# One decoder layer with a hierarchical mixture of experts: two more weight slots, a reordered routing step and a reordered expert stage

## The chip, the cores and the metric

The kernel runs on one core of one Trainium2 chip. The metric is the device time of one execution in microseconds (us); lower is better. A core has five engines, each with its own in-order instruction queue: PE (matmul, with its weight loads shown as PEld), DVE (vector), ACT (scalar, activation functions), POOL (GpSimd) and SP, which here only issues transfers (DMAs). Transfers run on 16 shared DMA engines.

## What is computed

One layer on 256 tokens of width 1024 in f32: an RMS norm and a combined projection, two attention branches, an output projection added to `x`, and then a mixture of 32 experts, of which each token uses two out of one group of eight. Every expert's three weight matrices are 1 MiB each, so the expert stage reads 96 MiB whatever the routing says.

```python
h = rms_norm(x, norm_attn);  proj = h @ w_in
merged = sig(gA) * (A @ w_o_mla) + sig(gB) * (Bd @ w_o_dil)   # two attention branches
x = x + merged @ w_out
h2 = rms_norm(x, norm_ffn)
gp = softmax(h2 @ w_rg + b_rg);  g_p, g_i = top_1(gp)         # group of experts
e_p, e_i = top_2(softmax((h2 @ w_re + b_re)[g_i]))            # two experts inside it
combine = one_hot(g_i * 8 + e_i) * g_p * e_p / sum(e_p)
for e in range(32):
    he = silu(h2 @ w_gate[e]) * (h2 @ w_up[e])
    y += combine[:, e] * (he @ w_down[e])
x = x + y
```

## The kernel before

The tokens are two blocks (`tb` 0 and 1) of 128, one token per partition. Every large operand is an SBUF tile of 128 x 2048 f32 (1 MiB), called a slot.

**Projections** (`w_in`, `w_o_*`, `w_out`) stream through four slots `ring`. ACT and POOL (or DVE) split each weight into a high part `wh` and a low part `wl`, and PE sums three products into PSUM banks `pj`. A planner (`Weave`) holds prices of the engines and decides while the program is written in which order the attention branches' instructions stand between these matmuls.

**Experts** are worked off in eight groups of four (`g`), with 32 token places (`SLOT`) for each expert; what is over goes through `overflow`. `moe_loads` lists the 96 weight loads in the order w_gate, w_up, w_down of each group. `release` hands a slot back and calls `pump`, which issues the next load into the slot that came free first. All these loads stand in one queue, SP's, in the order of the program; each waits there until its slot is no longer read. The slots are four `early` (released at 40 us of the planner's clock, `first_slots`), eight `side`, four `ring`, `hT0`, `oT`, `late_slot`, and four `xs` that take the place of the projection's tiles, when `release(*extra_slots)` comes: 23 slots in all. The first loads into slots of group 0 are made in two halves (`release_halves`).

**Between the two stages** stands the routing. `x_out(tb, half)` adds the output projection to `x1` and sums its squares; `x_turn` transposes it for the router's matmul `logits`; `out_rms` makes 1/rms by an integer first guess and three Newton steps, on POOL for block 0 and on DVE for block 1; `x_sorted` copies `x1` into `tok`, reordered; `route` is ten dependent DVE steps per block that end in `sel`; `ranks` and `slots_of` count places on PE and DVE, `one_hot` builds the selection matrix, and `gather` and `gathered` bring the chosen tokens into `xg`. `warm_up` puts matmuls without use between them.

**One group** is: 32 matmuls of w_gate and 32 of w_up into one bank `gu`; `activate` (tanh on ACT, two products on DVE) to `he`; two transposes of the combine weights and two of `he` into `tr`, copied to `trs`; the next group's gather; then `down` (w_down, into `pd` or `px`), a copy to `do`, and `combine`, which adds into the four banks `y`. In group 0 four matmuls also add the residual `x1` to `y`. In the last group w_down comes in three column pieces (`PIECES`: 512, 256 and 256 columns, both rows of each partition), and each finished piece of `y` is copied to `x1` and sent out by ACT's and SP's queues.

All instructions of PE, DVE, ACT and POOL are recorded by one helper, `Engine`, so that they carry one line number, L128; tiles tell them apart. Loads of SP have lines of their own: L337 projections, L212, L215 and L217 experts, L228 halves.

Of the kernel before, what the change touches and what calls it, by code (L numbers as in the profile page):

```python
# [14 lines left out]
I32 = mybir.dt.int32  # L15
# [44 lines left out]
TUNE = dict(gap=0.103, dV=0.05, dS=0.208, dG=0.121, dPE=0.257, early=-0.366, norm=0.02, split1=-0.463, split2=1.641, pace=2.246, small=9.132, masks=18.02, busy=6, first=40.0, space=0.0, busy2=0, busy3=4, rms=1.0, sines=14.0, route=7, route2=6)  # L60
# [82 lines left out]
def layer(ctx, tc, A, out):  # L143
# [17 lines left out]
    x1 = ct([P, 2, D], "x1")  # L161
    late_slot = ct([P, 2048], "late_slot")
    NRING, NSIDE, NEARLY = 4, 8, 4
# [32 lines left out]

    def down_piece(t, piece):

        c0, n = piece
        return t[:, 2 * c0:2 * (c0 + n)].rearrange("p (j n) -> p j n", j=2)  # L200

    def pump():
        while moe_loads:
            name, e, piece = moe_loads[0]
# [6 lines left out]
            if piece is None:  # L211
                SP.dma_start(t, expert_src(name, e))  # L212
            elif name == "w_up":
                cut = slice(piece[0], sum(piece))
                SP.dma_start(t[:, cut], expert_src(name, e)[:, cut])  # L215
            else:
                SP.dma_start(down_piece(t, piece),  # L217
                             A[name][0, e].rearrange("(p j) n -> p j n", p=P)[:, :, piece[0]:sum(piece)])
# [18 lines left out]
    with ExitStack() as c1:  # L237
# [433 lines left out]
        biases = [wt([P, 512], f"bias{b}") for b in range(2)]  # L671
# [307 lines left out]

        tok = ct([P, 2, 8, P], "tok")  # L980
# [35 lines left out]
        def out_rms(tb, E):  # L1016

            y, (v, t) = rstd2[:, tb:tb + 1], (wt([P, 1], f"{name}{tb}") for name in ("rs_vo", "rs_to"))
            E.tensor_scalar(v, sso[:, tb, 0:1], sso[:, tb, 1:2], EPS, op0=ALU.add, op1=ALU.add)
            yield  # L1020
            E.tensor_scalar(y.bitcast(I32), v.bitcast(I32), -0.5, 1597463007.0, op0=ALU.mult, op1=ALU.add)
            E.tensor_scalar(v, v, -0.5, None, op0=ALU.mult)
            yield
            for _ in range(3):
                E.tensor_scalar(t, y, y, v, op0=ALU.mult, op1=ALU.mult)
                yield
                E.tensor_scalar(y, t, 1.5, y, op0=ALU.add, op1=ALU.mult)
                yield
# [419 lines left out]
    with ExitStack() as c2:  # L1448
# [3 lines left out]
        release(*extra_slots)  # L1452
# [8 lines left out]
        pc = ys[3][:, :NE]  # L1461

        def weights():
# [6 lines left out]
            S.activation(wts[:, :, 2], wts[:, :, 2], AF.Exp)  # L1470
            V.scalar_tensor_tensor(wts[:, :, 3], wts[:, :, 2], 1.0, wts[:, :, 1], op0=ALU.add, op1=ALU.mult)
# [12 lines left out]
        def count_full():  # L1484
            for tb in range(2):
# [15 lines left out]
        def overflow():  # L1501
# [6 lines left out]
            with tc.If(n > 0):  # L1508
                with tc.For_i(0, n, 1) as it:
# [11 lines left out]
                    for tb in range(2):  # L1521
# [14 lines left out]
                        activate(he, gus)  # L1536
# [16 lines left out]
        def activate(he, gu):  # L1553

            S.activation(he, gu[:, 0], AF.Tanh, scale=0.5)
            V.scalar_tensor_tensor(he, he, 1.0, gu[:, 0], op0=ALU.add, op1=ALU.mult)
            V.tensor_tensor(he, he, gu[:, 1], op=ALU.mult)

        def gather_all():

            for q in range(2):
                tag = "pd" if q else "px"
                px = ps2.tile([P, 4, P], F32, name=tag, tag=tag, bufs=1)
                for tb in range(2):
                    gather(px, q, tb)
                gathered(px, q)
# [11 lines left out]
        count_full()  # L1578
        ov = out.rearrange("b (t p) d -> p (b t) d", p=P)
        for g in range(NGRP):  # L1580
            final = g == NGRP - 1
            if g == 4:
# [107 lines left out]
```

## Time and profile before

| | |
|---|---|
| time, median of 3 runs | 503.06 us (501.61 to 507.61) |
| the profiled execution: its time | 503.13 us |
| its span, first to last instruction | 501.3 us |
| PE busy | 455.0 us (91%) |
| DVE, ACT, POOL busy | 201.5, 174.1, 237.3 us |
| read from HBM | 144.00 MB |
| mean granted TensorE clock | 0.986 of full speed |

The time is the device's; the span covers the instructions alone, so the two differ by 1.83 us in the profiled execution. A busy PE isn't a PE at its peak, since ends of pipelined matmuls are modelled.

### The profile page before, as it was taken

The page shows a single profiled execution, that of the slowest core. Times are in us where ns is not written, and L with a number is a line of the kernel's source. Part 1 is how long each engine was busy: PE and PEld are TensorE (multiplying, and loading weights), DVE is VectorE, ACT ScalarE, POOL GpSimd, SP SyncE. Part 2 cuts the span into 40 slices and gives each one's busy share as a digit, 9 for nine tenths or more (in the row PEclk, how much of TensorE's full clock was granted, in tenths as well). Part 3 has the DMA queues.
Part 4 walks back from the last instruction along what each step waited for, and adds up shares of the span by engine and source line. Part 5 has one row for each costly group of instructions (what it writes and reads, how often), then busy time and mean ns, then how long its engine had stood idle before and what let it go on. Part 6 is the DMA issues. An engine that isn't in the chain of part 4 may idle for free.

```text
span 501.3 us, 8356 instructions
## 1 busy us (share of the span) xinstructions
PE 455.0 (91%) x3254; PEld 324.9 (65%) x3254; DVE 201.5 (40%) x477; ACT 174.1 (35%) x334; POOL 237.3 (47%) x293
## 2 busy tenths in 40 slices
PE   7898889999999999999999999897988887868876
PEld 4796778877878888788888886362635443425322
DVE  6455986478633521473434176122212121212001
ACT  6765465646646654565444330000000000000001
POOL 5898878885778697567798650000000000000000
PEclk9999999998999999999999999999999999997989
DMA  8676946552534256278987986999999999999995
GB/s 283 234 224 201 412 131 215 175 165 84 160 101 159 93 167 202 82 227 332 374 303 281 418 341 242 424 418 420 420 419 420 422 418 421 422 418 422 413 385 173
DMA packets 43955, 145.61 MB, mean 290 GB/s; under 512 B 5752, under 2 KB 11402, under 8 KB 33162
## 3 DMA queue, kind: packets, MB, share of 16 engines
q1 hardware_dynamic: 43194, 144.53, 76.2%
q8 instruction: 26, 0.43, 0.4%
q10 hardware_dynamic: 720, 0.53, 0.3%
q14 instruction: 15, 0.12, 0.1%
HBM read 144.00 MB, written 1.05 MB: 289 GB/s over the span
## 4 chain that ended last, share of the span: by engine, by line
PE 50%; DMA 34%; DVE 7%; POOL 5%; issue 1%; ACT 1%; SPq 1%; POOLq 0%; DVEq 0%; ACTq 0%
PE pj L128 36%; DMA xs<-in_w_up_dram 10%; PE pt L128 6%; DMA side<-in_w_gate_dram 4%; DMA ring<-in_w_gate_dram 4%; DMA side<-in_w_up_dram 4%; DMA oT<-in_w_down_dram 4%; POOL wl L128 3%; PE s L128 3%; DMA ring<-in_w_down_dram 3%; DMA early<-in_w_down_dram 2%; PE y L128 2%; DMA early<-in_w_gate_dram 2%; DVE late_slot L128 2%; DMA ring<-in_w_in_dram 1%; PE pd L128 1%
## 5 line engine op out<-in xcount | busy, mean ns | idle before, releaser
L128 PE MATMUL pj<-wh,hT 128*128 128x512 f32 (+2 forms) x576 | 191.0, 394 | 2.0 <-ACT wh L128 1.5
L128 POOL TENSOR_TENSOR wl<-ring,wh 128x512 fp32r<-128x512 f32 (+1 forms) x124 | 156.5, 1288 | 44.7 <-ACT wh L128 44.4
L128 PEld LDWEIGHTS pj<-wh,hT 128*128 128x128 f32 x576 | 109.6, 192 | 22.2 <-issue 2.2
L128 PE MATMUL pj<-wl,hT 128*128 128x512 f32 (+2 forms) x288 | 110.9, 385 | 2.9 <-POOL wl L128 2.5
L128 ACT ACTIVATE wh<-ring 128x1024 fp32r<-128x1024 f32 (+2 forms) x78 | 79.3, 1018 | 81.3 <-PE pj L128 64.7
L128 POOL TENSOR_TENSOR wc<-wc,comb 128x128 f32<-128x128 f32 x16 | 6.0, 398 | 170.7 <-DVE wc L128 170.7
L128 PEld LDWEIGHTS pj<-wl,hT 128*128 128x128 f32 x288 | 55.5, 193 | 11.4 <-POOL wl L128 3.6
L128 PE MATMUL gu<-side,xg 128*32 128x256 f32 x416 | 43.8, 400 | 4.7 <-DMA side<-in_w_up_dram 4.6
L128 ACT ACTIVATE he<-gu 128x256 f32<-128x256 f32 x8 | 3.1, 384 | 123.2 <-PE gu L128 123.2
L128 PE MATMUL y<-do,trs 128*128 128x512 f32 x56 | 27.8, 618 | 11.7 <-DVE do L128 6.6
L128 DVE SCALAR_TENSOR_TENSOR he<-he,gu 128x256 f32<-128x256 f32 x8 | 3.4, 421 | 79.0 <-ACT he L128 79.0
L128 POOL TENSOR_TENSOR side<-side,st 128x512 f32<-128x512 f32 (+2 forms) x32 | 30.8, 991 | 5.9 <-DVE st L128 5.9
L128 PEld LDWEIGHTS gu<-side,xg 128*32 128x32 f32 x416 | 21.5, 115 | 17.2 <-DMA side<-in_w_up_dram 6.4
L128 PEld LDWEIGHTS y<-do,trs 128*128 128x128 f32 x56 | 9.5, 189 | 31.1 <-DVE do L128 12.9
L128 PE MATMUL gu<-ring,xg 128*32 128x256 f32 x176 | 25.1, 380 | 0.0
L128 DVE COPY do<-px 128x512 f32<-128x512 f32 x7 | 4.8, 691 | 50.3 <-PE px L128 50.3
L128 DVE COPY side<-pt 128x512 f32<-128x512 f32 (+2 forms) x26 | 16.6, 645 | 18.9 <-PE pt L128 17.7
L128 DVE TENSOR_TENSOR wl<-ring,wh 128x1024 fp32r<-128x1024 f32 (+2 forms) x16 | 18.7, 1168 | 12.3 <-ACT wh L128 11.9
L128 PE MATMUL gu<-xs,xg 128*32 128x256 f32 x160 | 19.4, 412 | 4.5 <-DMA xs<-in_w_up_dram 4.5
L128 ACT ACTIVATE do<-pd 128x512 f32<-128x512 f32 x7 | 4.2, 597 | 52.3 <-PE pd L128 52.3
L128 PE MATMUL pj<-wh,oT 128*128 128x512 f32 x64 | 21.1, 398 | 0.0
L128 DVE CUSTOM_DVE_ANT_0 side<-s,side 128x512 f32<-128x512 f32 (+2 forms) x32 | 15.4, 519 | 13.2 <-PE s L128 12.8
(270 smaller groups left out, 737.7 us busy)
## 6 DMA issues: line engine op xcount, KB each, us to landing
ring<-in_w_in_dram SPq DMA_DIRECT2D x25, 1024.0 KB, 5.2
side<-in_w_up_dram SPq DMA_DIRECT2D x16, 1024.0 KB, 17.6
side<-in_w_gate_dram SPq DMA_DIRECT2D x10, 1024.0 KB, 18.5
early<-in_w_gate_dram SPq DMA_DIRECT2D x7, 1024.0 KB
side<-in_w_down_dram SPq DMA_DIRECT2D x6, 1024.0 KB, 5.1
ring<-in_w_gate_dram SPq DMA_DIRECT2D x6, 1024.0 KB, 17.0
xs<-in_w_up_dram SPq DMA_DIRECT2D x6, 1024.0 KB
xs<-in_w_down_dram SPq DMA_DIRECT2D x6, 1024.0 KB, 18.4
```

The source lines that it names most:

```text
L128: r = f(*args, **kw)
```

## The change

- **Slots.** A fifth `early` slot is released with the four, and `x1` becomes a slot after the `xs`. For that `tok` takes over what `x1` was read for later: the residual (now added in group 2, from `tok` in its sorted order) and the staging of the output; the two gate-bias tiles become parts of `tok` as well.
- **Routing.** `out_rms` makes its first guess as exp(-0.5 ln(v)) on ACT and one Newton step on DVE, for both blocks. POOL copies block 0 to `tok` as soon as each half is there; ACT copies both halves of block 1. The block-0 route stands ahead of the block-1 route on DVE. `warm_up` has 3 + 5 matmuls in place of 6 + 7. ACT loads a table ahead of `x_out` and another after the exps of `weights`.
- **Groups.** w_gate and w_up go to two banks; the silu and the combine weights follow w_gate, ahead of w_up; the next group's gather is halved; `count_full` (two matmuls and DVE work on overfull experts) moves from ahead of group 0 to group 1.
- **Last group.** w_up is loaded in cuts of 1024, 512 and 512 columns and w_down in cuts of 1024 (the first row of each partition whole), 512, 256 and 256; the first row's matmuls run for all columns, then the second row's by pieces. `busy` puts 9 useless matmuls into w_up and 4 around the transposes.

Up to the last four halves of the output projection the order on PE, DVE, ACT and POOL is unchanged; on SP one load is added there.

```diff
-    NRING, NSIDE, NEARLY = 4, 8, 4
+    NRING, NSIDE, NEARLY = 4, 8, 5
...
+    UP = ((0, D), (D, 512), (D + 512, 512))
-    for half in range(2):
-        for j in range(4):
-            moe_loads.append(("w_up", NE - 4 + j, (half * 1024, 1024)))
-    for piece in PIECES:
-        for j in range(4):
-            moe_loads.append(("w_down", NE - 4 + j, piece))
-
+    for name, cuts in (("w_up", UP), ("w_down", UP[:1] + tuple((D + c0, n) for c0, n in PIECES))):
+        for c0, n in cuts:
+            for j in range(4):
+                moe_loads.append((name, NE - 4 + j, slice(c0, c0 + n)))
...
-        def out_rms(tb, E):
-
-            y, (v, t) = rstd2[:, tb:tb + 1], (wt([P, 1], f"{name}{tb}") for name in ("rs_vo", "rs_to"))
-            E.tensor_scalar(v, sso[:, tb, 0:1], sso[:, tb, 1:2], EPS, op0=ALU.add, op1=ALU.add)
-            yield
-            E.tensor_scalar(y.bitcast(I32), v.bitcast(I32), -0.5, 1597463007.0, op0=ALU.mult, op1=ALU.add)
-            E.tensor_scalar(v, v, -0.5, None, op0=ALU.mult)
-            yield
-            for _ in range(3):
-                E.tensor_scalar(t, y, y, v, op0=ALU.mult, op1=ALU.mult)
-                yield
-                E.tensor_scalar(y, t, 1.5, y, op0=ALU.add, op1=ALU.mult)
-                yield
+        def out_rms(tb):
+
+            y, (b, v, t) = rstd2[:, tb:tb + 1], (wt([P, 1], f"{name}{tb}") for name in ("rs_bo", "rs_vo", "rs_to"))
+            sum0, sum1 = sso[:, tb, 0:1], sso[:, tb, 1:2]
+            V.tensor_scalar(b, sum0, EPS, None, op0=ALU.add)
+            yield
+            S.activation(y, sum1, AF.Ln, bias=b)
+            S.activation(y, y, AF.Exp, scale=-0.5)
+            V.tensor_tensor(v, sum1, b, op=ALU.add)
+            yield
+            V.scalar_tensor_tensor(t, y, -0.5, y, op0=ALU.mult, op1=ALU.mult)
+            yield
+            V.tensor_tensor(t, t, v, op=ALU.mult)
+            yield
+            V.scalar_tensor_tensor(y, t, 1.5, y, op0=ALU.add, op1=ALU.mult)
...
+        nc.scalar.preload_act_table_set("natural_log_exp_and_others")
         half_unit(n_last, (0,))
         x_out(0, 0)
+        x_sorted(0, 0, G)
         half_unit(n_last + 1, (0,))
         x_out(0, 1)
+        x_sorted(0, 1, G)
         x_turn(0, 0)
         half_unit(n_last, (1,))
         x_out(1, 0)
         x_turn(0, 1)
-        rms0 = out_rms(0, G)
+        half_unit(n_last + 1, (1,))
+        rms0, rms1, r0, r1 = out_rms(0), out_rms(1), route(0), route(1)
+        next(rms0)
+        next(rms0)
+        x_out(1, 1)
+        x_turn(1, 0)
+        next(rms1)
+        logits(0, 0)
         for _ in rms0:
             pass
+        x_turn(1, 1)
+        next(rms1)
         for half in range(2):
-            x_sorted(0, half, G)
-        half_unit(n_last + 1, (1,))
-        x_out(1, 1)
-        x_turn(1, 0)
-        logits(0, 0)
-        x_turn(1, 1)
-        x_sorted(1, 0, G)
-        x_sorted(1, 1, S)
+            x_sorted(1, half, S)
         logits(0, 1)
         bank = pj_bank()
         lg[1], pp[1] = bank[:, :NR], bank[:, 64:64 + NE]
...
         warm_up(pxs[1], TUNE["route2"])
-        rms1, r0, r1 = out_rms(1, V), route(0), route(1)
+        next(r0)
+        for _ in rms1:
+            next(r0)
         for _ in range(4):
-            next(rms1)
-        for _ in rms1:
             next(r0)
         for _ in r0:
             next(r1)
...
-        release(*extra_slots)
+        release(*extra_slots, x1.rearrange("p t d -> p (t d)"))
...
@@ -1458,7 +1456,13 @@
         for bank in ("pd", "gu", "tr", "px"):
             ps2.tile([P, 512], F32, name=bank, tag=bank, bufs=1)
 
-        pc = ys[3][:, :NE]
+        def busy(n):
+
+            dst = ps2.tile([P, 512], F32, name="pd", tag="pd", bufs=1)
+            for _ in range(n):
+                PE.matmul(dst, ones, ones[:, None, :].to_broadcast([P, 4, P]), start=True, stop=True,
+                          skip_group_check=True)
+
...
-        count_full()
+            if g == 1:
+                count_full()
...
-            gu = ps2.tile([P, 2, FF], F32, name="gu", tag="gu", bufs=1)
-            for i, name in ((0, "w_gate"), (1, "w_up")):
+            gate = ps2.tile([P, 2, FF], F32, name="gu", tag="gu", bufs=1)[:, 0]
+            up = ps2.tile([P, 512], F32, name="px", tag="px", bufs=1)[:, :FF]
+            trs = w2([P, 4, P], "trs")
+            he = w2([P, 512], "do")[:, :FF]
+            for name, dst in (("w_gate", gate), ("w_up", up)):
...
+                        if final and dst is up and j and k in (4, 6):
+                            busy(2 if k == 4 else 1)
+                        PE.matmul(dst[32 * j:32 * j + 32], xg[:, k, 32 * j:32 * j + 32], w[j][:, k],
+                                  start=k == 0, stop=k == 7, skip_group_check=True, tile_position=(0, 32 * j))
...
-            if g + 1 < NGRP:
-                one_hot(g + 1)
-            he = w2([P, FF], "he")
-            wc = combine_weights(g)
-            activate(he, gu)
-            tr = ps2.tile([P, 4, P], F32, name="tr", tag="tr", bufs=1)
-            for tb in range(2):
-                PE.transpose(tr[:, 2 + tb], wc[:, tb].rearrange("p e s -> p (e s)"), ident)
-            if g + 1 < NGRP:
-                gather_all()
+                if dst is gate:
+                    silu(he, gate)
+                    tr = ps2.tile([P, 4, P], F32, name="tr", tag="tr", bufs=1)
+                    if g:
+                        weigh(g, tr, trs)
+                    if g + 1 < NGRP:
+                        one_hot(g + 1)
+            V.tensor_tensor(he, he, up, op=ALU.mult)
             hf = he.rearrange("p (q j) -> p q j", j=2)
+            if final:
+                busy(2)
+            else:
+                gather_half(1)
+            if g == 0:
+                weigh(g, tr, trs)
             for j in range(2):
                 PE.transpose(tr[:, j], hf[:, :, j], ident)
-            trs = w2([P, 4, P], "trs")
-            V.tensor_copy(trs, tr)
+            if final:
+                busy(2)
+            V.tensor_copy(trs[:, :2], tr[:, :2])
+            if not final:
+                gather_half(0)
             dos = {}
-            if g == 0:
+            if g == 2:
                 for tb in range(2):
                     for half in range(2):
...
+                        PE.matmul(ys[2 * tb + half], ident,
+                                  tok[:, tb, :, half * 64:(half + 1) * 64].rearrange("p r q -> p q r"), start=False,
...
+            def down(bank, piece, jfs, start):
+
                 c0, n = piece
-                tag = "px" if i == 1 else "pd"
+                for jf in jfs:
+                    for j in range(4):
+                        w = at("w_down", j).rearrange("p (j n) -> p j n", n=D)[:, jf, c0:c0 + n]
+                        PE.matmul(bank[32 * j:32 * j + 32, c0 % 512:c0 % 512 + n], trs[:, jf, 32 * j:32 * j + 32], w,
+                                  start=start and jf == 0, stop=jf == 1, skip_group_check=True,
+                                  tile_position=(0, 32 * j))
...
-            pieces = PIECES if final else WHOLE
-            down(0, pieces[0])
-            if not final:
-                combine(pieces[0])
-            down(1, pieces[1])
+                    V.tensor_copy(do, src)
+
             if final:
-                combine(pieces[0])
-                combine(pieces[1])
-                down(2, pieces[2])
-            combine(pieces[-1])
+                banks = [ps2.tile([P, 512], F32, name=tag, tag=tag, bufs=1) for tag in ("pd", "px")]
+                for half in range(2):
+                    down(banks[half], WHOLE[half], (0,), True)
+                for i, piece in enumerate(PIECES):
+                    bank = banks[piece[0] // 512]
+                    if i == 2:
+                        combine(PIECES[0])
+                    down(bank, piece, (1,), False)
+                    rows_out(i, bank, piece)
+                combine(PIECES[1])
+                combine(PIECES[2])
+            else:
+                for i, (piece, tag) in enumerate(zip(WHOLE, ("pd", "px"))):
+                    bank = ps2.tile([P, 512], F32, name=tag, tag=tag, bufs=1)
+                    down(bank, piece, (0, 1), True)
+                    rows_out(i, bank, piece)
+                    combine(piece)
```

SP at the start of the expert stage, the loads that fill the slots ahead of group 0's halves (L212 and L228), before; the number behind a tile's name tells tiles of one name apart:

```order
L212 DMA ring_63<-in_w_up_dram 128x2048
L212 DMA xs_2640<-in_w_up_dram 128x2048
L212 DMA xs_2641<-in_w_down_dram 128x2048
L212 DMA xs_2642<-in_w_down_dram 128x2048
L212 DMA xs_2643<-in_w_down_dram 128x2048
L228 DMA early_78<-in_w_down_dram 128x1024
L228 DMA early_79<-in_w_gate_dram 128x1024
L228 DMA early_80<-in_w_gate_dram 128x1024
```

and now (L209 and L221; x is `x1`, `hT` and `ring` come ahead of these rows in both):

```order
L209 DMA ring_63<-in_w_up_dram 128x2048
L209 DMA ring_64<-in_w_up_dram 128x2048
L209 DMA xs_2634<-in_w_down_dram 128x2048
L209 DMA xs_2635<-in_w_down_dram 128x2048
L209 DMA xs_2636<-in_w_down_dram 128x2048
L209 DMA xs_2637<-in_w_down_dram 128x2048
L209 DMA x_58<-in_w_gate_dram 128x2048
L221 DMA early_79<-in_w_gate_dram 128x1024
```

One load more, into `x1`, stands between the `xs` and the halves, and what the `xs` hold has moved on by one matrix.

DVE in the routing, from block 0's group choice (`pen`) to the sum that selects its experts (`sel`), before:

```order
L128 TENSOR_TENSOR pen<-iota_u,gidx 128x4
L128 SCALAR_TENSOR_TENSOR el_lg<-pen,el_lg 128x32
L128 SCALAR_TENSOR_TENSOR el_lg<-pj,rstd_157,rbias 128x36
L128 MAX top<-el_lg 128x8
L128 MAX gtop<-el_lg 128x8
L128 MAX_INDEX idx<-top,el_lg 128x8
L128 MAX_INDEX gidx<-gtop,el_lg 128x8
L128 TENSOR_TENSOR pair<-iota_u,idx 128x64
L128 TENSOR_TENSOR pen<-iota_u,gidx 128x4
L128 TENSOR_TENSOR sel<-pair 128x32
```

and now:

```order
L128 TENSOR_TENSOR pen<-iota_u,gidx 128x4
L128 SCALAR_TENSOR_TENSOR el_lg<-pen,el_lg 128x32
L128 MAX top<-el_lg 128x8
L128 MAX_INDEX idx<-top,el_lg 128x8
L128 TENSOR_TENSOR pair<-iota_u,idx 128x64
L128 SCALAR_TENSOR_TENSOR el_lg<-pj,rstd_157,rbias 128x36
L128 TENSOR_TENSOR sel<-pair 128x32
```

Block 1's steps (`gtop`, `gidx`, the second `pen`) no longer stand between those of block 0.

PE in the last group, the end of the second down piece to the last piece's matmuls, before (`y` are the output banks, `xg` the copied piece):

```order
L128 MATMUL px<-early_81,trs 32x256
L128 MATMUL y_2648<-xg,trs 128x512
L128 MATMUL y_2650<-xg,trs 128x512
L128 MATMUL y_2649<-xg,trs 128x256
L128 MATMUL y_2651<-xg,trs 128x256
L128 MATMUL pd<-early_78,trs 32x256
L128 MATMUL pd<-early_79,trs 32x256
L128 MATMUL pd<-early_80,trs 32x256
L128 MATMUL pd<-early_81,trs 32x256
```

and now:

```order
L128 MATMUL px<-xs_2634,trs 32x256
L128 MATMUL y_2643<-xg,trs 128x512
L128 MATMUL y_2645<-xg,trs 128x512
L128 MATMUL px<-hT_2438,trs 32x256
L128 MATMUL px<-ring_63,trs 32x256
L128 MATMUL px<-ring_64,trs 32x256
L128 MATMUL px<-xs_2634,trs 32x256
L128 MATMUL y_2644<-xg,trs 128x256
L128 MATMUL y_2646<-xg,trs 128x256
```

The second piece's two matmuls into `y` have moved behind the last down piece, which has four matmuls in place of eight.

## Rows read from the trace of the kernel before

**Rows 1.** The page, DMA share and GB/s in 40 slices of the span

```profile
DMA  8676946552534256278987986999999999999995
GB/s 283 234 224 201 412 131 215 175 165 84 160 101 159 93 167 202 82 227 332 374 303 281 418 341 242 424 418 420 420 419 420 422 418 421 422 418 422 413 385 173
```

**Rows 2.** The chain that ended last: start us, us, engine and what

```profile
326.55 13.42 DMA ring<-in_w_down_dram
...
483.40 3.25 PE gu L128 x26
...
491.68 1.05 PE px L128 x10
492.73 2.78 PE y L128 x8
495.50 1.05 PE pd L128 x16
...
497.01 1.15 PE y L128 x4
498.18 0.42 DVE x L128
```

**Rows 3.** Windows: stretch, its length, busy PE, PEld, DVE, ACT, POOL, PEclk, DMA share, GB/s

```profile
70.00:75.00 5.00, 5.00 (x25) 4.24 (x24) 3.70 (x7) 3.15 (x8) 5.00 (x5) 1.00 0.35 92
289.00:292.00 3.00, 3.00 (x24) 2.69 (x23) 1.72 (x4) 1.78 (x4) 2.33 (x7) 1.00 0.44 128
302.00:306.00 4.00, 4.00 (x69) 2.72 (x71) 2.82 (x13) 0.77 (x5) 0.00 (x0) 1.00 0.09 24
360.00:400.00 40.00, 33.25 (x350) 17.09 (x352) 8.03 (x22) 1.58 (x3) 1.51 (x4) 1.00 1.01 420
```

**Rows 4.** Timeline of SP's queue: start us, us, line, what is issued

```profile
46.12 2.28 SPq L212 DMA_DIRECT2D early<-in_w_gate_dram  x4
57.15 66.78 SPq L337 DMA_DIRECT2D ring<-in_w_in_dram  x11
...
304.71 0.33 SPq L228 DMA_DIRECT2D early<-in_w_down_dram  x1
```

**Rows 5.** Windows of 1 us in the last group, columns as in rows 3

```profile
476.00:477.00 1.00, 1.00 (x21) 0.49 (x13) 0.00 (x0) 0.00 (x0) 0.00 (x0) 1.00 1.03 410
485.00:486.00 1.00, 1.00 (x9) 0.36 (x2) 0.00 (x0) 0.00 (x0) 0.00 (x0) 0.50 1.07 372
489.00:490.00 1.00, 0.68 (x8) 0.29 (x12) 0.26 (x1) 0.00 (x0) 0.00 (x0) 1.00 0.99 324
493.00:494.00 1.00, 1.00 (x3) 0.38 (x2) 0.19 (x1) 0.12 (x1) 0.00 (x0) 1.00 0.21 73
```

**Rows 6.** Timeline of routing and first gate: start us, us, engine, operation [idle before]

```profile
286.17 0.63 ACT L128 ACTIVATE xg<-x 128x512 f32<-128x512 f32 x1 [3.66 <-DVE x L128]
...
291.99 0.98 PE L128 MATMUL s<-wr,xT 128*128 128x36 f32 x8
...
292.24 3.27 POOL L128 COPY tok<-x 128x512 f32<-128x512 f32 x3
...
293.38 0.25 DVE L128 SCALAR_TENSOR_TENSOR el_lg<-s,rstd,rbias 128x36 f32<-128x36 f32 x1
...
294.45 1.11 DVE L128 SCALAR_TENSOR_TENSOR el_lg<-pen,el_lg 128x32 f32<-128x32 f32 x1
...
296.42 0.19 DVE L128 TENSOR_TENSOR sel<-pair 128x32 fp32r<-128x32 f32 x1
296.53 0.18 DVE L128 SCALAR_TENSOR_TENSOR el_lg<-pen,el_lg 128x32 f32<-128x32 f32 x1
...
302.77 3.66 PE L128 MATMUL gu<-early,xg 128*32 128x256 f32 x64
```

**Rows 7.** Groups of instructions on ACT: busy us, mean ns | idle before

```profile
L128 ACT ACT_TABLE_LOAD x2 | 2.6, 1283 | 0.0
```

**Rows 8.** DMA issues: count, KB each, median us from issue to landing

```profile
out_dram<-x SPq DMA_DIRECT2D x2, 128.0 KB, 1.7
```

More of the change, by code (lines that the diff above doesn't have):

```diff
@@ L57, in split_const @@
     return parts
-TUNE = dict(gap=0.103, dV=0.05, dS=0.208, dG=0.121, dPE=0.257, early=-0.366, norm=0.02, split1=-0.463, split2=1.641, pace=2.246, small=9.132, masks=18.02, busy=6, first=40.0, space=0.0, busy2=0, busy3=4, rms=1.0, sines=14.0, route=7, route2=6)
+TUNE = dict(gap=0.103, dV=0.05, dS=0.208, dG=0.121, dPE=0.257, early=-0.366, norm=0.02, split1=-0.463, split2=1.641, pace=2.246, small=9.132, masks=18.02, busy=6, first=40.0, space=0.0, busy2=0, busy3=4, rms=1.0, sines=14.0, route=5, route2=3)
 class Weave:
@@ L161, in layer @@
     x1 = ct([P, 2, D], "x1")
+    tok = ct([P, 2, 8, P], "tok")
     late_slot = ct([P, 2048], "late_slot")
-    NRING, NSIDE, NEARLY = 4, 8, 4
+    NRING, NSIDE, NEARLY = 4, 8, 5
     ring = [ct([P, 2048], f"ring{i}") for i in range(NRING)]
@@ L670, in layer @@
         bias_t = {}
-        biases = [wt([P, 512], f"bias{b}") for b in range(2)]
+        biases = [tok[:, 0, 4 * b:4 * b + 4].rearrange("p r q -> p (r q)") for b in range(2)]
         def gate_bias(b, half):
@@ L1484, in count_full @@
         def count_full():
+            pc = ps2.tile([P, 512], F32, name="pd", tag="pd", bufs=1)[:, :NE]
             for tb in range(2):
@@ L1551, in overflow, with silu, gather_half, weigh @@
             release(*ws)
[L1553 to L1563, printed above, removed]
-                for tb in range(2):
-                    gather(px, q, tb)
-                gathered(px, q)
+        def silu(he, gate):
+            S.activation(he, gate, AF.Tanh, scale=0.5)
+            V.scalar_tensor_tensor(he, he, 1.0, gate, op0=ALU.add, op1=ALU.mult)
+        def gather_half(q):
+            tag = "pd" if q else "px"
+            px = ps2.tile([P, 4, P], F32, name=tag, tag=tag, bufs=1)
+            for tb in range(2):
+                gather(px, q, tb)
+            gathered(px, q)
+        def weigh(g, tr, trs):
+            wc = combine_weights(g)
+            for tb in range(2):
+                PE.transpose(tr[:, 2 + tb], wc[:, tb].rearrange("p e s -> p (e s)"), ident)
+            V.tensor_copy(trs[:, 2:], tr[:, 2:])
         def combine_weights(g):
@@ L1628, in combine @@
                 for tb in range(2):
-                    PE.matmul(yv[tb], trs[:, 2 + tb], dos[piece], start=False, stop=final, skip_group_check=True)
+                    PE.matmul(yv[tb], trs[:, 2 + tb], dos[piece], start=g == 0, stop=final, skip_group_check=True)
                 if final:
                     sl = slice(c0, c0 + n)
-                    S.activation(x1[:, 0, sl], yv[0], AF.Copy)
-                    V.tensor_copy(x1[:, 1, sl], yv[1])
-                    nc.scalar.dma_start(ov[:, 0, sl], x1[:, 0, sl])
@@ L1635, in combine @@
-                    SP.dma_start(ov[:, 1, sl], x1[:, 1, sl])
-            def down(i, piece):
-                c0, n = piece
-                tag = "px" if i == 1 else "pd"
+                    S.activation(yo[:, 0, sl], yv[0], AF.Copy)
+                    V.tensor_copy(yo[:, 1, sl], yv[1])
+                    nc.scalar.dma_start(ov[:, 0, sl], yo[:, 0, sl])
+                    SP.dma_start(ov[:, 1, sl], yo[:, 1, sl])
+            def down(bank, piece, jfs, start):
+                c0, n = piece
+                for jf in jfs:
[4 more added lines that the diff above has]
+                                  tile_position=(0, 32 * j))
@@ L1640, in down, with rows_out @@
+            def rows_out(i, bank, piece):
+                c0, n = piece
                 do = xg.rearrange("p k t -> p (k t)")[:, c0:c0 + n] if final else w2([P, 512], "do")
                 dos[piece] = do
-                pd = ps2.tile([P, 512], F32, name=tag, tag=tag, bufs=1)
-                for jf in range(2):
-                    for j in range(4):
-                        w = at("w_down", j)
-                        w = down_piece(w, piece) if final else w.rearrange("p (j n) -> p j n", n=D)[:, :, c0:c0 + n]
-                        PE.matmul(pd[32 * j:32 * j + 32, :n], trs[:, jf, 32 * j:32 * j + 32], w[:, jf],
-                                  start=jf == 0, stop=jf == 1, skip_group_check=True, tile_position=(0, 32 * j))
+                src = bank[:, c0 % 512:c0 % 512 + n]
```

35 lines of the change are left out of this document (12 added, 23 removed).

## The prediction

> **What bounds the kernel now.** I read the page's slices first. In the last 40% of the span the DMA line is all nines, at about 420 GB/s, while the slices before it swing between 82 and 418 [rows 1]. Next the chain of waits: from 326.55 to 483.4 us it is transfers alone, each released by the one before, and only then PE, ACT and DVE of the last group [rows 2]. In that stretch PE is busy 33.25 of 40 us at full clock while the transfers stand at 1.01 of their engines [rows 3]: the expert stage waits for its weights. So I looked for holes in the transfers. The one that matters lies ahead of the stage: from 302 to 306 their share is 0.09 [rows 3], because all 23 slots are full and SP can issue only when group 0's first matmuls let a slot go, at 304.71 [rows 4]; bytes flow 1.3 us later. From there arithmetic sets the end: 73 loads of 1 MiB are left, at 2.5 us each (1.049 MB by 420 GB/s). A load made before 302 is worth 2.5 us; an earlier release is worth what it is earlier, as long as a hole is left. Behind this stands the tail: the last w_up lands at 483.4 and the end comes 17.9 us later, by a chain of computation, though w_down's traffic ends near 493.9, where the DMA share has fallen to 0.21 [rows 2, 5].
>
> **The fifth early slot: 2.5 us.** Its load is issued at about 48 us behind the other four [rows 4]; it costs SP one issue of some 0.5 us and the transfers 2.5 us, in a stage with room (share 0.35 from 70 to 75 us [rows 3]). Queued behind it on SP is the next `ring` load, which waited for its slot until 57.15 anyway [rows 4]; four ring slots stand between a load and its use, so I take zero, with 2.5 us as the upper end if the ring ran dry.
>
> **The slot in `x1`: 2.5 us.** It is free when ACT's copies to `tok` end, which I place at 293.4 to 295.7, behind ACT's Ln and Exp. Its load stands on SP behind the `xs` and ahead of the halves, so it carries the transfers from about 302.2 to 304.7, into the hole. Were the copies 7 us later it would hold up the halves queued behind it. Ends: 0 and 2.5; I take 2.5, since the hole is 3.8 us wide.
>
> **Routing: 0.65 us.** Block 0's selection `sel` came at 296.42 [rows 6]. One step ahead of it shows a cost that goes: masking block 0's logits took 1.11 us and ended with POOL's three copies (292.24 + 3.27 = 295.51), while the same step for block 1, after them, took 0.18 [rows 6]. Now POOL is through with its copies before 289: 0.9 us less. Against it, block 0's router matmuls end only at 292.97 [rows 6], so the faster 1/rms moves the first `el_lg` just from 293.38 to about 293.05; and block 1's Newton step waits for ACT's Exp near 293.4, with block 0's DVE steps queued behind that wait. Walking DVE's new order at 0.2 us per dependent step gives `sel` at 295.75, 0.65 earlier. Block 1 no longer runs between block 0's steps and ends later, so its gather gains only 0.5; the count matmuls in front of the first gate are gone. First gate matmul: 302.1 in place of 302.77 [rows 6]; first release 304.05. Ends: -0.4 (block 1 bound by ACT) and 1.2. The transfers then run to 304.7 and start again at 305.35: a hole of 0.65 stays, so these three terms add, and no more than 0.65 is left to win here. The first table load (1.28 us [rows 7]) lies in 3.66 us of idle ACT [rows 6]; the second has from about 304 until the gate's end near 305.8.
>
> A rule bears on the moved copies. The Trainium skill (SBUF — State Buffer, "SBUF: two separate sides") says that DVE and GpSimd have a port pair in common which one of them holds for a whole instruction, and that of DVE's operations only those with two SBUF inputs or in a two-port mode compete for it. The masking step reads two SBUF tiles and waited; `el_lg` at 293.38, from PSUM, took 0.25 beside the same copies [rows 6]: the trace agrees. The copies now stand beside `x_out`, which reads PSUM and one SBUF tile: nothing by the rule; were one `x_out` held up as the masking step was, it would be 0.9 late and the sum up to 0.65 smaller.
>
> **Experts' groups: 0.** Four residual matmuls, `count_full` and the silu move inside stages where PE has 6.7 idle us in 40 [rows 3]; the transfers hide that. If this cover were gone, see the third rival.
>
> **Tail: 0.55 us.** The rates of the last windows are 410 GB/s with cuts of 1024 columns, 372 with 512, 324 with 256 [rows 5]. w_up's second half, now in 512s, lands 0.5 later. w_down needed 10.5 us behind the last w_up (483.4 to 493.9); by those rates its old cuts make 12.1 (2.1 MB at 372, 2.1 at 324) and the new ones 11.15 (2.1, 1.05, 1.05), so I scale 10.5 to 9.7. The same scaling puts the old second piece at 491.1; PE got it at 491.68 [rows 2], so 0.6 is added for the signal. With 5.65 from the terms above, the last w_up lands at 483.4 - 5.65 + 0.5 = 478.25, w_down's second column piece 8.3 + 0.6 later at 487.15, the last at 488.55. The work between (some 5 matmuls, product, transposes, copy, first rows) is done by about 483.5 at full clock and waits for w_down. From 487.25 PE bounds: four matmuls of 256 columns 0.53 (half of 1.05), `y` of the first piece 1.7 and of the second 0.85 (with start-up 2.78 together), last piece 0.53, its `y` 1.15 [rows 2]: 492.0. Copy and wait 0.45, then 2.7 us from the copy's end to the span's end as before (498.6 to 501.3 [rows 2]): 495.1. Ends: -0.3 and 1.9 (PE waits for nothing).
>
> **Sum.** 2.5 + 2.5 + 0.65 + 0.55 = 6.2; 501.3 - 6.2 = 495.1. The profiled execution took 1.83 us more than its span, and its 503.13 stands at the median of the runs (503.06): **496.9 us**, 1.2% faster. A change of 2%, about what a measurement of this kernel can tell from no change, would be 10 us.
>
> **Rivals.** *No hole for `x1`*: its copies or the `xs` come late, or the release does, and the second slot and the routing give nothing: 3.15 us back, 500.1. For it: nearly all of the gain there is to be had in 4 us of one window. Chance 0.14.
>
> *Half clock in the tail.* After PE had waited for w_up its clock was 0.50 at 485 [rows 5], that is 1.2 GHz. The filling matmuls speak against it, the waits for w_down's cuts for it. With the PE terms doubled the first rows are ready at 486.4, the end comes at 500.7, the time is 502.5. Chance 0.1.
>
> *Slower: PE becomes the bound of the expert stage.* One group's weights take 30 us, PE's work about 25. w_up's bank is now also that of a gather and of the second down piece, and `do` holds the silu's result too: each reuse makes PE or ACT wait for a reader. From 5 us more per group on, every further one counts seven times: 2 us over is 14 against 6.2 gained, 510.9. Against it: the first 5 us are free, and the clock was full [rows 3]. Chance 0.04.
>
> *Small cuts signal later.* A 128 KB transfer took 1.7 us from issue to landing [rows 8], 0.3 of it bytes. If each of w_down's cuts signals 1.4 behind its traffic in place of 0.6, PE's last stretch starts 0.8 later: 497.7. Chance 0.08. The Trainium skill (DMA: Bandwidth & Descriptors, "Anatomy of one DMA") gives about 2.0 us of fixed cost for a transfer, most of it between the last byte and the signal; by that, an estimate, the time is 498.3. No row here shows the fixed cost by itself.
>
> *More than forecast.* Routing gains 1.3, the hole closes, and PE waits for nothing in the tail: 501.3 - 5 - 1.3 - 1.9 = 493.1, time 494.9; 492.6 if the gap at 289 to 292 (share 0.44 [rows 3]) closes as well. Chance 0.08.
>
> **How the numbers follow.** The forecast keeps 0.56; its own range is 495.3 to 498.3. To hold 8 in 10 the range takes in late signals and the lost slot, with a margin for the spread of runs: 493.5 to 500.7. Faster by over 2% 0.07; slower by over 2% 0.04; within 2% 0.89.
>
> **What would show it.** Right: 25 loads issued ahead of the first half-load, at most 1 us without transfers before 306, nines from then on, the last w_up landing near 478, the first gate matmul near 302.1, PEclk 1.0 from 478 on. Wrong: the masking step still at 1 us, a hole of 3 us, w_up landing as before, PE busy above 29 of 30 us in a group, or an end more than 17 us behind the last w_up.

## The result, and the profile after

| | kernel before | changed kernel |
|---|---|---|
| time, median | 503.11 us (14 runs) | 506.5 us (14 runs, 504.1 to 509.31) |
| ratio to the kernel before | | 1.0057, 95% interval 1.0032 to 1.0083 |
| profiled execution: time, span | 503.13, 501.3 us | 504.1, 502.3 us |
| mean granted TensorE clock | 0.986 | 0.986 |

The change made the kernel 0.6% slower, where 1.2% faster was forecast; 506.5 lies above the range. Every ratio below is to the kernel before on the same chip, so that kernels are compared by their ratios; 0.01 is 5 us. One execution of no_fill (1150.26 us) and one of wc_early (579.1 us) were far longer than all others of their kernels and are in neither the ratios nor the medians below.

The page of the changed kernel, TensorE's clock and the transfers in 40 slices, answers to [rows 1]:

```profile
PEclk9999999999999999999999998999999989999989
DMA  8676966553524267268987999999999999999972
GB/s 285 230 224 204 419 201 216 174 168 114 144 86 166 88 187 238 77 236 326 373 294 291 402 358 359 423 421 419 420 420 421 418 421 418 421 419 417 340 273 84
```

The sixth slice (201, before 131) has the fifth early load, and the hole ahead of the expert stage is smaller (25th slice: 359, before 242; from 300 to 305 us the share is 0.92). So the two loads came in where they were forecast, and the routing ends earlier: the first gate matmul runs at 299.50 in place of 302.77, the first half-load goes out at 301.44 in place of 304.71 [rows 4, 6]. Some 1.7 us of this is not the change's (see the routing below). Timelines of DVE (the masking step of block 0, then `sel`), PE and SP of the changed kernel:

```profile
292.60 0.19 DVE L128 SCALAR_TENSOR_TENSOR el_lg<-pen,el_lg 128x32 f32<-128x32 f32 x1
...
293.66 0.18 DVE L128 TENSOR_TENSOR sel<-pair 128x32 fp32r<-128x32 f32 x1
...
299.50 0.85 PE L128 MATMUL gu<-early,xg 128*32 128x256 f32 x12
...
301.44 1.89 SPq L221 DMA_DIRECT2D early<-in_w_gate_dram  x3
```

What was gained there is gone by the end of the last group. The chain that ended last was transfers from 326.55 to 483.4 us in the kernel before [rows 2]. In the changed kernel the chain, which reaches back some 100 us, holds no transfer: it is PE's own order, with ACT, DVE and POOL in its waits. Its last group (start us, us, what):

```profile
471.86 3.63 PE gu L128 x64
...
475.51 0.39 ACT do L128
...
475.93 0.42 DVE do L128
476.35 0.21 DVE wc L128
...
476.69 0.41 POOL wc L128
...
477.15 0.33 PE tr L128
...
477.83 3.60 PE px L128 x34
481.44 0.95 PE pd L128 x2
482.39 0.55 PE px L128 x2
482.94 0.67 PE pd L128 x2
...
488.18 0.98 PE px L128 x10
489.16 0.66 PE pd L128 x2
...
499.16 0.42 DVE tok L128
```

w_gate ends at 475.5, and then PE stands until 477.15: the transposes of the combine weights `wc` come next in its queue. `wc` needs nothing of w_gate, but its comparison stands in DVE's queue behind the silu, which waits for tanh on ACT, and POOL's product follows the comparison. Then w_up takes 11.3 us (477.83 to 489.16), where the 64 matmuls of the group before took 3.59. PE's waits, by what ended them (us in all, times, longest), of the changed kernel and then of the kernel before:

```profile
PE tr L128 <- POOL wc L128: 13.9, 8, 1.8
PE y L128 <- DVE do L128: 7.0, 7, 1.3
PE y L128 <- ACT do L128: 5.0, 7, 0.7
...
PE tr L128 <- DVE trs L128: 0.5, 1, 0.5
```

```profile
PE pd L128 <- DVE trs L128: 7.7, 7, 1.1
PE y L128 <- DVE do L128: 6.6, 7, 1.0
PE y L128 <- ACT do L128: 5.1, 7, 0.8
PE gu L128 <- DMA side<-in_w_up_dram: 4.6, 3, 1.9
PE gu L128 <- DMA xs<-in_w_up_dram: 4.5, 5, 1.9
```

The wait for `trs` (1.1 in each of seven groups) was changed for one of 1.7 to 1.8 for `wc`, and no wait for an expert's load is left. How full an engine that sets the end looks, is seen in one group of each kernel (windows, columns as in [rows 3]), of before and then of after; the later rows are on the clock:

```profile
349.85:371.64 21.79, 18.96 (x205) 10.30 (x204) 4.71 (x12) 0.98 (x2) 0.76 (x2) 1.00 1.01 419
...
450.00:455.00 5.00, 2.78 (x19) 0.98 (x23) 0.00 (x0) 0.00 (x0) 0.00 (x0) 0.50 1.02 423
```

```profile
425.50:449.00 23.50, 19.64 (x209) 10.36 (x212) 4.87 (x13) 0.98 (x2) 0.76 (x2) 1.00 1.01 420
...
478.00:480.00 2.00, 2.00 (x32) 1.09 (x25) 0.29 (x1) 0.00 (x0) 0.00 (x0) 0.65 1.02 418
480.00:482.00 2.00, 2.00 (x12) 0.81 (x4) 0.00 (x0) 0.00 (x0) 0.00 (x0) 0.50 1.04 399
```

In the group of before PE waited for no load at all, and yet was busy 18.96 of 21.79 us: the other 2.83 are waits for its own results (`trs` 1.15, `do` 0.72 and 0.96), and transfers cover none of that. 21.8 us is PE's own pace. With it the stretch from the first to the last gate can be parted. Before: 302.77 to 473.11, 170.3 us, of which PE's pace makes 25.3 (group 0, with the residual) and six times 21.8, in sum 156.1; 14.2 us are left, the room that the loads leave PE (below: the cover). Waits that loads ended are 9.4 of it; the rest stands between and behind these waits, where w_up's matmuls ran two at a time and the clock fell (0.50 from 450 to 455 us). After: 299.50 to 471.79, 172.3 us, with no wait for a load. The 16.2 above 156.1 are 3.5 in the residual's matmuls (7.07 us for 3.60), 3.4 at the half clock (windows at 310 and 405 with 0.66 and 0.69), and 9.3 in the groups, 1.3 each.

So PE came to the last w_up at 477.8, just when its last cut landed (issued at 471.48; loads of w_up in that stretch took 5.7 to 6.3 us in the median). The transfers ended just behind 487 us (share 0.10 from 487 to 488, then none; the last piece was forecast for 488.55), but nothing waited for them any more, and 24.5 us of tail stood behind 477.8.

### The profile page after: what moved, and what is told of

Read it like the earlier page. It is cut to its first block, busy times and chain, and to the rows that moved or that the text cites. A ratio compares the mean times of both kernels' runs of the same rounds, so it can differ in the third digit from the quotient of the medians.

```text
span 502.3 us, 8374 instructions
## 1 busy us (share of the span) xinstructions
PE 461.7 (92%) x3254; PEld 325.4 (65%) x3254; DVE 204.2 (41%) x486; ACT 178.4 (36%) x341; POOL 233.6 (47%) x283
## 5 line engine op out<-in xcount | busy, mean ns | idle before, releaser
L128 ACT ACTIVATE do<-gu 128x256 f32<-128x256 f32 x8 | 3.1, 384 | 75.5 <-PE gu L128 64.8
L128 PE MATMUL px<-side,xg 128*32 128x256 f32 x160 | 28.4, 399 | 0.0
L128 ACT ACTIVATE side<-side,st 128x512 f32<-128x512 f32 (+2 forms) x32 | 18.4, 578 | 4.4 <-DVE st L128 4.4
L128 DVE SCALAR_TENSOR_TENSOR do<-do,gu 128x256 f32<-128x256 f32 x8 | 3.4, 421 | 38.9 <-ACT do L128 38.9
L128 PE MATMUL tr<-ident,wc 128*128 128x128 f32 x16 | 5.2, 328 | 14.1 <-POOL wc L128 13.9
L128 PE MATMUL s<-side,side 64*128 64x128 f32 (+2 forms) x160 | 15.9, 294 | 0.9 <-DVE st L128 0.8
```

Of the source, the lines that this page charges most:

```text
L128: r = f(*args, **kw)
```

## Experiments

**Theory 1**: the new wait, with the residual, brings PE to the last w_up so late that nothing covers the tail, whose fills and clock then count. **Theory 2**: the fills of the tail alone. **Theory 3**: the transfers (new cuts, new slots).

**no_fill.** The changed kernel without `busy`:

```diff
-                        if final and dst is up and j and k in (4, 6):
-                            busy(2 if k == 4 else 1)
...
-            if final:
-                busy(2)
-            else:
+            if not final:
                 gather_half(1)
...
-            if final:
-                busy(2)
```

> The changed kernel (504.1 us in its profile) without the 13 filling matmuls of the last group. Theory 1 (PE itself sets the end now: the wait for the combine weights ahead of w_up and the residual's strided read hold PE up in every group, so that it comes to the last w_up no earlier than its weights land, at 477.8, and the fills then stand in the path): PE still starts the last w_up near 477.8, w_up ends near 482 in place of 489.2, the end comes some 6.5 us earlier: 497 to 498. Theory 2 (the fills alone, the wait is harmless): the same 497 to 498. Theory 3 (PE waits for transfers: the new cuts or slots): PE only waits instead, 504.

500.71 us, ratio 0.9942 (0.992 to 0.9964): 1.1% or 5.8 us below the changed kernel, against theory 3. (The times expected of no_fill, weigh_late, resid and slots23 count from the profiled execution's 504.1, 2.4 below the median, so it is differences that compare: here 6.5 us were expected.) PE still starts w_up at 477.74 and now waits 0.5 us each for `do` and `trs` and 0.4 for the first copied piece; the fall of the clock at 475 to 485 stays. In the chain of the changed kernel the eight pieces of fills are 4.7 us. Besides, a fill parts the matmuls of the four column strips, which otherwise run side by side: two between fills take 0.55, 64 in a row 3.59, and the 30 behind the first fill take 2.5 us more than their part of that. Less the 1.4 of waits that the fills covered these are 5.8 of the 6.1 by which the spans differ (502.3 and 496.2).

**weigh_late.** The transposes go behind w_up; the products of the combine weights stay:

```diff
-                    if g:
-                        weigh(g, tr, trs)
+                    wc = combine_weights(g)
...
-            if g == 0:
-                weigh(g, tr, trs)
+            weigh(wc, tr, trs)
```

> The changed kernel with the two transposes of the combine weights behind w_up and the half gather, as its group 0 has them; their products stay where they are on DVE and POOL. Theory 1: the wait of 1.7 to 1.8 us for POOL goes from seven groups, PE's group takes 21.8 us as before in place of 23.1, PE comes to the last w_up some 9 us earlier and waits there for the weights, which land near 477.5; the fills run inside that wait, and the end comes near 493.5 in the span, time 495. Theory 2: the fills still cost their 6 us, only the last wait counts: 502. Theory 3: 504.

496.23 us, ratio 0.9867 (0.9822 to 0.9913): 1.9% below the changed kernel, with all fills in place. Its gates come 21.8 us apart (321.40, 343.19), as in the kernel before. The chain of weigh_late is again one of transfers up to the last group, and PE's timeline shows it waiting for w_up in the last two groups; no window of 5 us up to 490 is below full clock:

```profile
436.25 19.72 DMA side<-in_w_down_dram
...
456.03 15.00 DMA side<-in_w_up_dram
471.03 0.04 issue
471.07 1.92 PE px L128 x28
```

```profile
446.09 3.64 PE L128 MATMUL px<-early,xg 128*32 128x256 f32 x58 [1.85 <-DMA early<-in_w_up_dram]
...
469.78 0.62 PE L128 MATMUL px<-ring,xg 128*32 128x256 f32 x2 [0.18 <-DMA ring<-in_w_up_dram]
471.07 0.40 PE L128 MATMUL px<-side,xg 128*32 128x256 f32 x1 [0.67 <-DMA side<-in_w_up_dram]
```

w_up ends at 480.42, 8.7 us earlier than with the wait; the span is 494.5, where 493.5 was expected here and the prediction's sum gave 495.1.

**wc_early.** PE's order is untouched, but the products are written ahead of the group's w_gate, so that nothing is left to wait for:

```diff
             at = lambda name, j: moe_at[name, 4 * g + j]
+            wc = combine_weights(g)
...
-                        weigh(g, tr, trs)
+                        weigh(wc, tr, trs)
```

> The changed kernel with PE's order untouched, the combine weights' transposes between w_gate and w_up as the change has them, but their products written ahead of the group's w_gate, so that DVE and POOL are through with them before PE comes there. If it is the wait for POOL that costs (theory 1), PE's group falls from 23.1 to some 21.3 us, transfers set the end and the time is that of weigh_late: 495.5 to 497. If the place itself costs (a break between w_gate and w_up, or the waits that follow), 501 or more.

498.09 us, ratio 0.9912 (0.9883 to 0.9941): 1.4% below the changed kernel, 1.1 us above theory 1's range, with an interval that meets that of weigh_late. The wait for `wc` is left once (0.94 us, group 1), a group takes 21.3 us (371.33 to 392.60), and the place in PE's queue costs nothing that is clear of the noise: the wait does. Coming earlier only lengthens the waits for loads (2.3 in weigh_late for the first row here), and behind them the clock is at 0.50 from 445 to 450 in its profile:

```profile
PE px L128 <- DMA early<-in_w_up_dram: 3.8, 3, 1.8
...
PE tr L128 <- POOL wc L128: 0.9, 1, 0.9
```

**fill_wait.** Four useless matmuls stand in each wait of the changed kernel:

```diff
             wc = combine_weights(g)
+            if g:
+                busy(4)
             for tb in range(2):
```

> The changed kernel with four useless matmuls (1.7 us) in PE's queue inside each wait for the combine weights, so that PE works through the wait, which stays as long. It parts the wait's time from what it does to TensorE's clock. If the clock's falls to 1.2 GHz (310, 405 and 475 to 485 us in the changed kernel's profile, some 5 us in sum) come from the waits, they go: PE comes to the last w_up some 3 us earlier and w_up runs at full clock: 501 to 502. If only the wait's time counts, nothing changes: 506.

503.2 us, ratio 1.0004 (0.9984 to 1.0024): 0.5% below the changed kernel, somewhat less than expected. PE comes to the last w_up at 477.70 as before, but at full clock, which the windows of fill_wait show:

```profile
478.00:480.00 2.00, 2.00 (x35) 0.97 (x27) 0.23 (x1) 0.00 (x0) 0.00 (x0) 1.00 1.02 399
480.00:482.00 2.00, 2.00 (x8) 0.84 (x8) 0.00 (x0) 0.00 (x0) 0.00 (x0) 1.00 1.01 368
```

All ten executions have a mean clock of 0.992 to 0.999, those of the changed kernel 0.979 to 0.989. So of the 1.9% that the wait costs, about a quarter is what it does to the clock and the rest its time; the intervals leave that share wide.

**resid.** The residual's matmuls read `tok` in its stored order and write the columns apart:

```diff
-                        PE.matmul(ys[2 * tb + half], ident,
-                                  tok[:, tb, :, half * 64:(half + 1) * 64].rearrange("p r q -> p q r"), start=False,
+                        PE.matmul(ys[2 * tb + half].rearrange("p (q r) -> p r q", r=8), ident,
+                                  tok[:, tb, :, half * 64:(half + 1) * 64], start=False,
```

> The changed kernel with the residual's four matmuls of group 2 reading tok in its stored order and writing the columns apart in PSUM, in place of reading them apart. Theory 1: they took 6.9 us in place of 3.6 because the read is strided; if the strided write is free, PE comes to the last w_up 3.3 us earlier, waits there for the weights and has that much of the fills covered: some 3 us less, 501. If the strided write costs as much as the read: 504. Theories 2 and 3: 504 either way.

503.12 us, ratio 0.9994 (0.9962 to 1.0026): 0.6% or 3.2 us below the changed kernel, as theory 1 had it. The profiled execution shows the shorter matmuls, not the gain: two more falls of the clock (0.66 from 330 to 335 and from 355 to 360 us) take it up, and its last gate comes at 471.46. Timelines of the changed kernel and of resid:

```profile
361.17 7.07 PE L128 MATMUL y<-tok,ident 128*128 128x512 f32 x8
```

```profile
364.33 3.60 PE L128 MATMUL y<-tok,ident 128*128 128x512 f32 x8
```

**slots23.** The changed kernel with the slots of before:

```diff
-    NRING, NSIDE, NEARLY = 4, 8, 5
+    NRING, NSIDE, NEARLY = 4, 8, 4
...
-        release(*extra_slots, x1.rearrange("p t d -> p (t d)"))
+        release(*extra_slots)
```

> The changed kernel with 23 slots as in the kernel before (no fifth early slot, x1 not released). Theory 1: the transfers come 5 us later, the last w_up lands near 482.5 in place of 477.5, PE's start of it moves by no more than that and the fills run in the waits: some 1 to 3 us slower than the changed kernel, 505 to 507. Theory 2: the same. Theory 3 (transfers set the end): the full 5 us, 509; and if the slots themselves did the harm, 502 or less.

506.78 us, ratio 1.006 (1.0034 to 1.0085): the same as the changed kernel, where theory 1 had 1 to 3 us more. Two slots are worth nothing in it, which speaks against theory 3.

**late_23.** The edits of weigh_late and of slots23 together.

> The order of weigh_late (496.2 us) with 23 slots in place of 25. Theory 1: with the wait gone the transfers set the end again, so two slots are worth two loads of 2.5 us, less what PE's waits in the tail hide: 500 to 501.5. If PE's order still set the end, slots would be worth nothing, as they were in slots23: 496 to 497.

501.52 us, ratio 0.9981 (0.9962 to 1.0001): 1.1% or 5.7 us above weigh_late. The same two slots are worth their two loads as soon as PE waits for loads again; the last w_up but one shows it (PE's timeline of late_23, against 1.85 once in weigh_late):

```profile
447.15 0.62 PE L128 MATMUL px<-side,xg 128*32 128x256 f32 x2 [1.85 <-DMA side<-in_w_up_dram]
449.63 6.50 PE L128 MATMUL px<-side,xg 128*32 128x256 f32 x58 [1.86 <-DMA side<-in_w_up_dram]
```

**before_wait.** The kernel before with the wait alone:

```diff
+                if i == (0 if g else 1):
+                    he = w2([P, FF], "he")
+                    S.activation(he, gu[:, 0], AF.Tanh, scale=0.5)
+                    V.scalar_tensor_tensor(he, he, 1.0, gu[:, 0], op0=ALU.add, op1=ALU.mult)
+                    wc = combine_weights(g)
+                    tr = ps2.tile([P, 4, P], F32, name="tr", tag="tr", bufs=1)
+                    for tb in range(2):
+                        PE.transpose(tr[:, 2 + tb], wc[:, tb].rearrange("p e s -> p (e s)"), ident)
...
-            wc = combine_weights(g)
-            activate(he, gu)
...
+            V.tensor_tensor(he, he, gu[:, 1], op=ALU.mult)
```

> The kernel before with one thing of the change: silu and combine weights between w_gate and w_up (from group 1 on), so that PE waits some 1.8 us there. From its trace: between the first and the last gate PE has 170.3 us, of which its own pace makes 25.3 + 6 x 21.8 = 156, so 14.3 us of waits for loads cover 7 x 1.8 = 12.6. If the cover is one sum over the stage (theory 1) the time stays within 1 or 2 us, up to 506 with falls of the clock. If each wait counted by itself, 515. If the cover were the 5 us for each group of the prediction, 503 and no change whatever the clock does.

506.95 us, ratio 1.0094 (1.0058 to 1.013): 1 us above the most that theory 1 gave, far from 515, and not the 503 of a cover for each group. The wait is 1.9, but a group grew from 21.8 to 24.4 us (327.43, 351.84, 376.23): 2.6 each, of which 0.7 is not explained here, 18 in seven, more than the 14.2 of cover. The profiled execution, the fastest of six with 501.3 us of span, shows the balance: PE waits for no load, its last w_up starts at 484.35, and the last part of w_up ran from 483.40 in the kernel before [rows 2]. Other executions have lower clocks (0.979 to 0.989) and are up to 6.7 us longer. In the changed kernel a group grew by only 1.3, since its order also took the wait for `trs` away.

```profile
PE tr L128 <- POOL wc L128: 14.7, 8, 1.9
PE pd L128 <- DVE trs L128: 7.7, 7, 1.1
```

**late_nofill.** The edits of weigh_late and no_fill together.

> The order of weigh_late (496.2 us) without the 13 filling matmuls of the last group. Its chain has PE busy without a break from 471.1 to 482, the fills 3.9 us of it, while the last w_up lands near 477.2 and w_down's last cut near 487: without fills w_up ends near 478.5 in place of 480.4, and the end is set by w_down's last cut: 1 to 1.5 us less, 495. If PE's waits for the cuts bring the clock to 1.2 GHz, as the kernel before had it at 485 (0.50), the last stretch takes longer: 498 to 500.

496.31 us, ratio 0.9876 (0.9846 to 0.9905): the same as weigh_late. The fills, which cost 1.1% or 5.8 us where PE is late, are worth nothing either way where it waits. The gain of 1 us did not come, and the clock did not fall.

**late_resid** and **late_few.** weigh_late with the edit of resid; and that with three fills in w_up in place of nine (`k == 4`, one each).

> weigh_late (496.2 us) with the residual's matmuls as in resid. In resid, where PE sets the end, the 3.4 us that they save brought 506.5 to 503.1. Theory 1: here PE waits for loads in the last two groups, so the same 3.4 us only lengthen those waits: 496 to 496.5. If PE still set the end in part, 493 to 495.

> late_resid with 3 fills among the last w_up's matmuls in place of 9. With 9 PE worked from 471.1 to 482 without a break, with none the time was the same (496.3), so transfers set the end at either number: 495.5 to 496.5. If the fills' time and the clock's falls had cancelled there, a number between them gives less: 494.5.

497.61 us, ratio 0.9884 (0.9856 to 0.9912), and 497.12 us, 0.9881 (0.9851 to 0.9911): neither is to be told from weigh_late. The 3.5 us of the residual, worth 3.2 in resid, are hidden here. No version beats weigh_late, which beats both kernels.

## Why the prediction was wrong

**The step that failed is "Experts' groups: 0", with the cover that it named.** It read PE's 6.7 idle us in 40 [rows 3] as room that transfers leave. Of these 5.6 were waits for PE's own results on ACT and DVE, 0.3 was a wait for a load, and for 0.8 the profile names nothing; the loads left PE 14.2 us in the whole stretch, all of it from 393 us on, and none in a group like 349.85 to 371.64. The silu and the combine weights ahead of w_up were priced at nothing, since DVE, ACT and POOL are nearly idle there; but PE's queue is in order, and a short chain over three idle engines between two blocks of matmuls stops it for as long as the chain is: 1.7 us. Taking that wait away by place or by time brings the ratio from 1.0057 to 0.9867 and 0.9912. The residual's matmuls, priced at nothing by the same cover, took 7.07 us in place of 3.60 and were worth 3.2 us (resid). Of the signs of being wrong one came: the end stood 24.5 us behind PE's start of the last w_up, where the sign was 17 behind its landing.

**The third rival had the mechanism, at the wrong place and from the wrong point.** It let the first 5 us of each group be free, as one group's loads take 30 us and PE 25 (its own pace is 21.8). But two groups lie in the slots at the start; loads and PE run out of step, and the cover is one sum over the stage. The faster start and the extra slots drew on the same sum: each load made earlier takes as much from it. It was used up after 1.3 us a group, the residual and the clock, and from there on the tail counted in full. That is also why the loss is only 3.4 us, not the 14 of the rival. Its sign, PE busy above 29 of 30 us in a group, did not come (19.64 of 23.50) and couldn't: an engine held up by its own chain is the bound without being full.

**Slots: right, where they can count.** Forecast 5.0; 5.7 us between late_23 and weigh_late, nothing between slots23 and the changed kernel. The hole from 302 to 306 (share 0.09) is gone.

**Routing: right in kind, too small.** The masking step took 0.19 in place of 1.11 as forecast. The first gate came 3.27 earlier for 0.65, but some 1.7 of that is a fall of the clock at 115 us in the profiled execution of the kernel before (last section). before_wait, whose code is that of before up to there, has no such fall and its first gate at 301.05, 1.55 behind the changed kernel's 299.50; slots23, with the change's routing, has such a fall and its first gate at 300.94, 1.83 ahead of 302.77. So the routing gave some 1.6 to 1.8, beyond the upper end of 1.2.

**Tail: its premise failed, and where the sum came out that was in part luck.** "The work between is done by about 483.5 and waits for w_down" fails in the changed kernel, whose w_up ends at 489.16. weigh_late ends within 0.6 us of the span forecast, but not that way either: in PE's timeline behind 471.07 only `trs` holds it up, no piece of w_down, and the second column piece starts at 485.46, where the forecast had 487.25:

```profile
481.82 0.50 PE L128 MATMUL tr<-ident,do 128*128 128x128 f32 x2 [0.52 <-DVE trs L128]
...
485.46 0.38 PE L128 MATMUL px<-hT,trs 128*32 128x256 f32 x1
```

No run isolates the rival of late signals. The section that it quotes for 2.0 us (the Trainium skill, DMA: Bandwidth & Descriptors, "Anatomy of one DMA") is headed as the path of transfers that GpSimd issues; the loads here are issued by SP.

**Half clock in the tail** came true (0.65 and 0.50 from 478 to 482), but behind a wait for POOL, not for w_up; it is worth some 0.5% with all other falls (fill_wait), and its 502.5 is near the profile's 504.1 by chance.

## What to carry to other kernels

Before calling an engine's idle time room, ask what ended each piece of it: what its own dependent chain ends is pace, and only waits for the other resource are cover, one sum for the whole stage. An instruction moved forward in an in-order queue must be costed by when its operands are ready there, even if every engine in that chain is idle. Filling matmuls and gains on the other resource are worth something only on the side that waits: here the same fills cost 5.8 us or nothing, and the same two slots gained 5.7 us or nothing.

## What the runs showed of the hardware

By the groups of instructions, a matmul of 512 f32 columns that are read 512 bytes apart from SBUF (`tok` with its eight rows innermost) took 1039 ns in the mean (changed kernel), and 592 with the columns side by side (kernel before); written 32 bytes apart into PSUM it took 592 as well (resid). The Trainium skill (SBUF — State Buffer, "Door 1: The DMA port swizzle") says that each access that crosses to another 16-byte line of SBUF costs more, and that any non-contiguous access of PSUM slows a matmul much. The first half agrees with these rows; the second isn't seen in this write.

Waits of 1.5 to 1.9 us on PE were followed by stretches at 1.2 GHz in some groups and not in others (0.66 from 310, 0.69 from 405 and 0.65 from 478 us in the changed kernel, none behind the waits that end at 330.06 and 431.00), and in fill_wait, with matmuls without use in the wait, the falls at 405 and 478 us are gone. Such falls differ between executions even where the instructions are the same: the window at 115 us of the kernel before and of before_wait, below, and with it their first gates, 1.7 us apart. A difference of that size ahead of a change is not the change's.

```profile
115.00:120.00 5.00, 5.00 (x20) 4.04 (x20) 3.90 (x17) 2.96 (x12) 2.87 (x6) 0.66 0.05 20
```

```profile
115.00:120.00 5.00, 5.00 (x31) 4.34 (x29) 4.88 (x20) 4.19 (x14) 3.21 (x7) 1.00 0.02 9
```
